# A block substitution emitted in pinned steps, and a longer filler tile, in a hybrid decoder layer

## The chip, the cores and the metric

The kernel runs on one core of a Trainium2 chip. The metric is the device time of one execution in microseconds. The profile calls the engines PE (TensorE), DVE (VectorE), ACT (ScalarE), POOL (GpSimd) and SP (SyncE).

## The reference

One decoder layer on 512 tokens of width 2048, float32:

```python
u = rms_norm(x, norm1_w);  proj = u @ w_in            # 2048 x 6160
conv_out = conformer_conv_group(proj[..., :2048])     # 8 channel groups x 128: GLU, causal depthwise conv (31), LayerNorm, silu
dn_out = gated_deltanet_group(proj[..., 2048:])       # 8 heads x 128, chunked delta rule
h = x + concat(conv_out, dn_out) @ w_out
h = h + square(relu(rms_norm(h, norm2_w) @ w_mlp_up)) @ w_mlp_down   # 2048 -> 8192 -> 2048
y = rms_norm(h, final_norm_w)
```

Inside the delta rule each head needs, for every chunk, the inverse of a unit lower triangular matrix:

```python
a = where(strict, (k_beta @ k.T) * decay, 0)
t_mat = triangular_solve(eye + a, eye, left_side=True, lower=True, unit_diagonal=True)
```

## The kernel before

**Numbers.** Each large product is made of three matmuls (`mm3`, lines 163 to 165): both operands are split into a high part (`hi`, rounded to the fp32r format, a copy on ScalarE) and a low part (`lo`, the rest, a subtraction on VectorE), and high x high, high x low and low x high are added in PSUM. The operand named `lhsT` is the stationary one, of 128 x 128; `rhs` is the moving one, of 128 x 512. In the views of the profile a matmul reads `out<-moving,stationary`.

**Stages.** (1) x is normalised and transposed into `u_h`, `u_l`. (2) The mixers: `ORDER` (line 28) is a list of column tiles. Each letter makes one or more input tiles of 128 columns of `proj` (`in_tile`, results `pin_k`, `pin_q`, ...): K is a head's key tile, C a conv group (two tiles), H a head's query and value tiles (and its gate tile z, if it hasn't been made), Z a gate tile, I the inversion for four heads. I0 serves heads 0 to 3, I1 heads 4 to 7. (3) `w_out` (results `po`), four column blocks. (4) The MLP in 16 blocks of 512: `up_block` (results `pu`, stationary the weights `whi_u`, `wlo_u`, moving the activations) alternates with `down_block` of the block before (results `px`, `py`, stationary the activations `sh`, `sl`, moving the weights `whi_d`, `wlo_d`). (5) The last block's product (`pl`, stationary `hh`, `hl`) and the final norm.

**Order of the mixers.** TensorE goes through the input tiles one after another. The other work of the mixers is written as Python generators, which sit in a list `pending`; every second group of three matmuls in `in_tile` calls `advance()`, which lowers each generator's counter by one and runs it on to its next `yield n` when the counter is used up. An input tile has 16 groups, so 8 advances. So each piece of a head's or a conv group's work is traced behind a certain matmul of a certain tile. In `delta_head` the pauses are `Y_PTQ = 10` until the query is transposed and `rt` is made, `Y_PX2 = 1`, four of `S1 = 1`, eight of `S2 = S3 = 1`, then `osum`, `ors` and `o` (lines 671 to 677), then `Y_POT = 4` until the transposes `pot` (line 681). Heads 0 and 4 take their block inverses later, after `Y_PTQ` and `Y_PX = 4`. In `conv_group` `crs` comes 20 + `Y_CPT` = 34 advances after the start.

Each engine has one queue and takes it in order. The queues' order is fixed before the run by a scheduler, which takes an instruction once it believes its inputs ready, by its own estimates, and of several the one traced first; `ahead()` counts an instruction as traced 600 earlier. `pin` (`tc.keep_in_program_order`) puts an instruction behind the one that was traced before it on the same engine.

**The inversion.** `invert_blocks` (lines 491 to 516) inverts the diagonal blocks of 32 x 32 of four heads at once, on GpSimd: `na` goes to DRAM and comes back as `inv_a`; 31 steps (`j` = 0 to 30) of one multiply (line 511) and one add (line 513) substitute forward; four transfers (line 515) put the result into `blk_out`. It is called at I0 and I1 and is traced there in one piece, 62 compute instructions in a row, none of them pinned. `block_inverse` (line 518) reads it back for a head as `yc` and spreads it into `y` and `xx`.

**Memory.** Tiles take their place in a partition of SBUF pool by pool, in the order in which the pools are opened, each padded to 32 bytes. The pool const begins at byte 16,544 of a partition, actp (`u`, `m`, `v`) at 18,112, wp (the weights) at 83,648, small at 128,704. Its first tile is `small_filler`, which nothing reads or writes. Behind small come rowp (130,592), mixc, inv and tmp; when the mixers are closed, h1p and mlp take their place (mlp from 163,360, with `sh`, `sl`, `hh`, `hl`, and the raw weights `wd`).

Of the kernel before, what the change touches and what calls it, by code (L numbers as in the profile page):

```python
# [8 lines left out]
F32 = mybir.dt.float32  # L9
# [5 lines left out]
P = 128  # L15
SEQ = 512
NT = SEQ // P
# [9 lines left out]
HB = 4  # L27
# [19 lines left out]
def tile_hybrid_block(ctx: ExitStack, tc: tile.TileContext, x, norm1_w, w_in, b_glu, dw_w, dw_b,  # L47
                      ln_g, ln_b, dn_conv_w, a_log, dt_bias, dn_norm_w, w_out, norm2_w, w_up,
                      w_down, final_w, out):
    nc = tc.nc  # L50
# [10 lines left out]
    dram = ctx.enter_context(tc.tile_pool(name="scratch", bufs=2, space=bass.MemoryType.DRAM))  # L61
# [2 lines left out]
    ps_aux = aux_banks.enter_context(tc.tile_pool(name="ps_aux", bufs=4, space=PSUM))  # L64

    small = ctx.enter_context(tc.tile_pool(name="small", bufs=4))
    small.tile([P, 8], F32, tag="small_filler", bufs=1, name="small_filler")

    mixers = ExitStack()
    row_pool = mixers.enter_context(tc.tile_pool(name="rowp", bufs=1))  # L70
# [4 lines left out]
    def tt(tag, name, shape=(P, NT, P), dtype=F32, bufs=1):  # L75
        return tmp.tile(list(shape), dtype, tag=tag, name=name, bufs=bufs)
# [54 lines left out]
    r = 0  # L131
    for v in (norm2_w, b_glu, dw_b, ln_g, ln_b, dn_norm_w):
        n = v.shape[1] // P
# [132 lines left out]
    pin = tc.keep_in_program_order  # L266

    def drain(kind):
        for p in list(pending):
            if p[2].startswith(kind):  # L270
                pending.remove(p)
                for _ in p[0]:
                    pass

    def start(kind, gen):
        drain(kind)
        pending.append([gen, next(gen), kind])
# [13 lines left out]
    def in_weights(col, j, name, sub=nc.vector, first=False):  # L291
        return load_pair(w_in[j * 1024:(j + 1) * 1024, col:col + P]
                         .rearrange("(k p) c -> p k c", p=P), [P, 8, P], f"{name}{j}", sub, first)
# [27 lines left out]
    def decay_products(pabT, toks):  # L321
        for k in range(KT):
            nc.tensor.matmul(pabT[:32, toks], lhsT=ab_w[:, k].rearrange("p a b -> p (a b)"),
                             rhs=uT[k][0][:, toks], start=(k == 0), stop=False)
            nc.tensor.matmul(pabT[:16, toks], lhsT=ab_w[:, k, 0], rhs=uT[k][1][:, toks],
                             start=False, stop=(k == KT - 1))
# [111 lines left out]
    def ahead():  # L438

        return tc.high_priority(offset=600)  # L440
# [49 lines left out]

    def invert_blocks(bt, keys):

        n = HB * NT * 4
        size, step = P * NT * P, 32 * NT * P + 32
        src = dram.tile([HB, 4 * step], F32, tag="blk_in", name=f"blk_in{bt}")
        dst = dram.tile([HB * 4, 32, NT, 32], F32, tag="blk_out", name=f"blk_out{bt}")
        a = inv_pool.tile([n, 32, 32], F32, tag="inv_a", name=f"inv_a{bt}")
        for i, key in enumerate(keys):
            nc.gpsimd.dma_start(src[i, :size].rearrange("(s t c) -> s t c", t=NT, c=P), key[2])
        diag = (src.rearrange("h (b r) -> (h b) r", r=step)[:, :step - 32]  # L500
                .rearrange("q (s t c) -> q t s c", t=NT, c=P)[:, :, :, :32])
        for t in range(NT):
            nc.gpsimd.dma_start(a[t * 4 * HB:(t + 1) * 4 * HB], diag[:, t])
        g = inv_pool.tile([n, 32, 32], F32, tag="inv_g", name=f"inv_g{bt}")
        nc.gpsimd.memset(g, 0.0)
        nc.gpsimd.memset(g.rearrange("n s c -> n (s c)")[:, 0:1024:33], 1.0)
        for j in range(31):
            w = 31 - j
            tm = inv_pool.tile([n, 256], F32, tag="inv_t", bufs=1, name=f"inv_t{bt}_{j}")
            tv = tm[:, :(j + 1) * w].rearrange("n (m i) -> n m i", i=w)  # L510
            nc.gpsimd.tensor_mul(tv, a[:, j:j + 1, j + 1:].to_broadcast([n, j + 1, w]),
                                 g[:, :j + 1, j:j + 1].to_broadcast([n, j + 1, w]))
            nc.gpsimd.tensor_add(g[:, :j + 1, j + 1:], g[:, :j + 1, j + 1:], tv)
        for t in range(NT):
            nc.gpsimd.dma_start(dst[:, :, t], g[t * 4 * HB:(t + 1) * 4 * HB])
        return dst

    def block_inverse(h, blocks):

        y = tt("y", f"y{h}")  # L520
        yc = tt("yc", f"yc{h}", (P, NT, 32))
        b0 = h % HB * 4
        with ahead():
            read = nc.gpsimd.dma_start(yc, blocks[b0:b0 + 4].rearrange("b s t c -> (b s) t c"))
            if h != HB - 1:
                pin(read)
            nc.gpsimd.tensor_mul(y.rearrange("p t (b c) -> p t b c", c=32),
                                 yc.unsqueeze(2).to_broadcast([P, NT, 4, 32]),
                                 block_mask.unsqueeze(1).unsqueeze(3).to_broadcast([P, NT, 4, 32]))


        xx = tt("xx", f"xx{h}")
        with ahead():
            nc.gpsimd.memset(xx, 0.0)
        for block, col in ((0, 0), (2, 32), (0, 64), (1, 96)):
            rows = slice(32 * block, 32 * block + 32)
            pin(nc.vector.transpose(xx[rows, :, col:col + 32], yc[rows]))
        return y, xx

    def delta_head(h, key, blocks, pq, pvv):  # L540
        e_c, e_s, e_l = (eg[:, i, :, h] for i in range(3))
        k, dec, na, kn, br = key
        late = h % HB == 0
        if not late:
            y, xx = block_inverse(h, blocks)
        q = tt("q", f"q{h}")
        short_conv(pq, 0, h, "q", q)
        v = tt("v", f"v{h}")
# [7 lines left out]
        def query_scales():  # L556
            nc.vector.tensor_scalar(ss, ss, EPS, None, ALU.add)
            rt = small.tile([P, NT], F32, tag="rt", bufs=2, name=f"rt{h}")
            with ahead():
                nc.gpsimd.tensor_tensor(rt, ss, neg_half[:, 0:NT], ALU.pow)  # L560
            cq = small.tile([P, 2, NT], F32, tag="cq", bufs=2, name=f"cq{h}")
            nc.vector.tensor_scalar(cq[:, 0], rt, P ** -0.5, None, ALU.mult)
            nc.vector.tensor_mul(cq[:, 1], cq[:, 0], e_c)
            return cq
# [21 lines left out]
        if late:  # L586
            yield Y_PX
            cq = query_scales()
            y, xx = block_inverse(h, blocks)
            yield Y_XX  # L590
        else:
            yield Y_PX2

        for b in (32, 64):
# [3 lines left out]
            for t in range(NT):  # L598
                pin(nc.tensor.matmul(pp[lo:, t], lhsT=na[:m, t, lo:], rhs=xx[:m, t, x0:x0 + 64],
                                     start=True, stop=True))  # L600
# [92 lines left out]
    keys = [None] * NH  # L693
    gates = [None] * NH
    blocks = [None] * (NH // HB)
    for op in ORDER.split():
        kind, r = op[0], int(op[1])
        if kind == "A":

            pabT = ps_mm.tile([P, SEQ], F32, tag="mm", name="pabT")  # L700
            pk = ps_mm.tile([P, SEQ], F32, tag="mm", name="pin_k0")
            ws = [in_weights(C_K, j, "k0", nc.gpsimd, True) for j in range(2)]
            for i in range(2):
                toks = slice(256 * i, 256 * i + 256)
                decay_products(pabT, toks)
                if i:
                    beta, glog_split, eg = decay_columns(pabT)
                for k in range(KT):
                    w = ws[k // 8]
                    mm3(pk[:, toks], (w[0][:, k % 8], w[1][:, k % 8]),  # L710
                        (uT[k][0][:, toks], uT[k][1][:, toks]), start=(k == 0), stop=(k == KT - 1))
        elif kind == "K":
            if r:
                pk = in_tile(C_K + r * P, f"k{r}", nc.gpsimd if r < NPK else nc.vector)
            start(f"key{r}", head_keys(r, pk))
        elif kind == "I":
            drain("key")
            blocks[r] = invert_blocks(r, keys[r * HB:(r + 1) * HB])
        elif kind == "C":
            pa = in_tile(C_CONF + r * P, f"a{r}")  # L720
            start("conv", conv_group(r, pa, in_tile(C_GATE + r * P, f"g{r}")))
        elif kind == "Z":
            drain("head")
            gates[r] = z_gate(in_tile(C_Z + r * P, f"z{r}"), r)
        else:
            pq = in_tile(C_Q + r * P, f"q{r}")
            pvv = in_tile(C_V + r * P, f"v{r}")
            start("head", delta_head(r, keys[r], blocks[r // HB], pq, pvv))
            if gates[r] is None:
                gates[r] = z_gate(in_tile(C_Z + r * P, f"z{r}"), r)  # L730

# [14 lines left out]
    def h1_row(t, dc):  # L746
        return h1[t // 2][dc][:, t % 2]
# [12 lines left out]
    for dc in range(4):  # L760
        ds = slice(dc * 512, (dc + 1) * 512)
        ps = [ps_mm.tile([P, SEQ], F32, tag="mm", name=f"po{dc}{t}") for t in range(NT)]
        for r in range(NH):
            w = load_pair(w_out_v[r, :, :, ds], [P, 2, 512], f"o{dc}{r}")
# [5 lines left out]
            for t in range(NT):  # L770
                cs = slice(t * P, (t + 1) * P)
                for i in range(2):
                    m = mixT[r + NG * i]
                    mm3(ps[t], (m[0][:, cs], m[1][:, cs]), (w[0][:, i], w[1][:, i]),
                        start=(r == 0 and i == 0), stop=(r == NH - 1 and i == 1))
# [176 lines left out]
    for fb in range(NFB):  # L952
        if fb < NFB - 1:
            a = mlp.tile([P, 4, 2, 256], F32, tag="quarters", name=f"a{fb}")
# [31 lines left out]
    for i in range(2):  # L986
        f = w_pool.tile([P, 2, 512], F32, tag="wraw", bufs=3, name=f"fw{i}")
# [5 lines left out]
    for t in range(NT):  # L993
        cs = slice(t * P, (t + 1) * P)
        for dc in range(4):
            ps = ps_mm.tile([P, SEQ], F32, tag="mm", name=f"pl{t}{dc}")
            for k in range(4):
                mm3(ps, (last[k][0][:, cs], last[k][1][:, cs]), last_w[4 * dc + k],
                    start=(k == 0), stop=(k == 3))
            h = h1_row(t, dc)  # L1000
# [6 lines left out]
        for c in (1, 0, 3, 2):  # L1007
            h = h1_row(t, c)
# [33 lines left out]
```

## Time and profile before

| | us |
|---|---|
| median of 3 runs (lowest, highest) | 2228.21 (2224.97, 2228.22) |
| the profiled execution | 2226.59 |
| its span, first to last instruction | 2224.5 |
| TensorE busy in it | 2177.6 |
| VectorE, ScalarE, GpSimd busy | 1527.8, 814.8, 203.1 |

The span is one profiled execution; the profiled execution's own time holds 2.1 us more, around it. Matmuls overlap each other and their durations include their way through the array, so a matmul of 390 ns doesn't keep the next one waiting for as long. What the engine was waiting for is read from the waits and the timelines, and how close matmuls follow each other from their starts.

### The profile page before, as it was taken

The page shows a single profiled execution, that of the slowest core. Times are in us where ns is not written, and L with a number is a line of the kernel's source. Part 1 is how long each engine was busy: PE and PEld are TensorE (multiplying, and loading weights), DVE is VectorE, ACT ScalarE, POOL GpSimd, SP SyncE. Part 2 cuts the span into 40 slices and gives each one's busy share as a digit, 9 for nine tenths or more (in the row PEclk, how much of TensorE's full clock was granted, in tenths as well). Part 3 has the DMA queues.
Part 4 walks back from the last instruction along what each step waited for, and adds up shares of the span by engine and source line. Part 5 has one row for each costly group of instructions (what it writes and reads, how often), then busy time and mean ns, then how long its engine had stood idle before and what let it go on. Part 6 is the DMA issues. An engine that isn't in the chain of part 4 may idle for free.

```text
span 2224.5 us, 25989 instructions
## 1 busy us (share of the span) xinstructions
PE 2177.6 (98%) x10073; PEld 1788.5 (80%) x10073; DVE 1527.8 (69%) x1956; ACT 814.8 (37%) x1349; POOL 203.1 (9%) x265
## 2 busy tenths in 40 slices
PE   6999999989999999999999999999999999999998
PEld 6887888768888788888888888888888888888886
DVE  6658678567668334567767767767767768767775
ACT  5433433423344223323323333333333333333342
POOL 3472102621110000000000000000000000000000
PEclk9999999989999999999999999999999999999999
DMA  5333233322223632233333332332332332333332
GB/s 162 103 98 91 68 88 81 86 73 78 77 78 82 202 96 85 85 105 95 104 105 94 107 106 91 111 107 86 114 104 86 114 104 87 112 104 92 108 123 77
DMA packets 189768, 220.66 MB, mean 99 GB/s; under 512 B 9901, under 2 KB 108622, under 8 KB 189646
## 3 DMA queue, kind: packets, MB, share of 16 engines
q1 hardware_dynamic: 188238, 215.34, 33.4%
q0 software_dynamic: 1408, 3.67, 0.6%
q8 instruction: 79, 1.29, 0.2%
q14 instruction: 43, 0.35, 0.0%
HBM read 212.17 MB, written 6.82 MB: 98 GB/s over the span
## 4 chain that ended last, share of the span: by engine, by line
PE 89%; DVE 5%; POOL 3%; issue 1%; DMA 1%; ACT 1%; SPq 0%; POOLq 0%; DVEq 0%; ACTq 0%
PE pu L164 10%; PE pu L163 10%; PE pu L165 10%; PE px L164 5%; PE px L165 5%; PE px L163 5%; PE py L164 4%; PE py L165 4%; PE py L163 4%; PE po L165 2%; PE po L163 2%; PE po L164 2%; DVE cacc L390 2%; PE pin_a L163 1%; PE pin_a L164 1%
## 5 line engine op out<-in xcount | busy, mean ns | idle before, releaser
L164 PE MATMUL pu<-v_l,whi_u 128*128 128x512 f32 x1024 | 399.6, 390 | 0.0
L163 PE MATMUL pu<-v_h,whi_u 128*128 128x512 f32 x1024 | 399.5, 390 | 0.0
L165 PE MATMUL pu<-v_h,wlo_u 128*128 128x512 f32 x1024 | 399.0, 390 | 0.0
L874 DVE TENSOR_TENSOR wlo_d<-wd,whi_d 128x1024 fp32r<-128x1024 f32 x180 | 218.5, 1220 | 255.3 <-ACT whi_d L873 255.3
L873 ACT CAST whi_d<-wd 128x1024 fp32r<-128x1024 f32 x180 | 188.9, 1049 | 467.5 <-PE pu L164 283.4
L163 PEld LDWEIGHTS pu<-v_h,whi_u 128*128 128x128 f32 x1024 | 192.2, 188 | 42.2 <-issue 0.2
L165 PEld LDWEIGHTS pu<-v_h,wlo_u 128*128 128x128 f32 x1024 | 192.3, 188 | 41.1 <-issue 0.2
L164 PEld LDWEIGHTS pu<-v_l,whi_u 128*128 128x128 f32 x1024 | 192.2, 188 | 40.5
L157 ACT CAST whi_u<-wraw_u 128x1024 fp32r<-128x1024 f32 x128 | 134.6, 1052 | 208.9 <-PE py L165 78.8
L164 PE MATMUL px<-wlo_d,sh 128*128 128x512 f32 x480 | 190.1, 396 | 0.0
L165 PE MATMUL px<-whi_d,sl 128*128 128x512 f32 x480 | 190.1, 396 | 0.0
L163 PE MATMUL px<-whi_d,sh 128*128 128x512 f32 x480 | 190.0, 396 | 0.0
L390 DVE SCALAR_TENSOR_TENSOR cacc<-chh,dw_cols,cacc 128x511 f32<-128x511 f32 (+14 forms) x240 | 180.7, 753 | 6.1 <-ACT cacc L387 2.7
L158 DVE TENSOR_TENSOR wlo_u<-wraw_u,whi_u 128x1024 fp32r<-128x1024 f32 x128 | 155.9, 1218 | 41.4 <-ACT whi_u L157 41.4
L891 DVE TENSOR_TENSOR h<-px,h 128x1024 f32<-128x1024 f32 x120 | 146.6, 1222 | 34.1 <-PE px L165 33.9
L164 PE MATMUL py<-wlo_d,sh 128*128 128x512 f32 x360 | 142.6, 396 | 0.0
L165 PE MATMUL py<-whi_d,sl 128*128 128x512 f32 x360 | 142.6, 396 | 0.0
L163 PE MATMUL py<-whi_d,sh 128*128 128x512 f32 x360 | 142.5, 396 | 0.0
L891 DVE TENSOR_TENSOR h<-py,h 128x1024 f32<-128x1024 f32 x90 | 110.1, 1223 | 28.6 <-PE py L165 26.8
L176 POOL TENSOR_TENSOR rs_rf<-rs_sf,neg_half 128x1 f32<-128x1 f32 x4 | 2.2, 542 | 1331.0 <-DVE rs_sf L174 1331.0
L165 PEld LDWEIGHTS px<-whi_d,sl 128*128 128x128 f32 x480 | 90.3, 188 | 21.8
L164 PEld LDWEIGHTS px<-wlo_d,sh 128*128 128x128 f32 x480 | 90.4, 188 | 21.7
(304 smaller groups left out, 4099.9 us busy)
## 6 DMA issues: line engine op xcount, KB each, us to landing
wraw_u<-in_w_mlp_up SPq DMA_DIRECT2D x128, 512.0 KB, 3.7
wd<-in_w_mlp_down SPq DMA_DIRECT2D x120, 512.0 KB, 3.7
wraw_o<-in_w_out SPq DMA_DIRECT2D x32, 512.0 KB, 4.3
wraw_k<-in_w_in SPq DMA_DIRECT2D x16, 512.0 KB, 4.0
wraw_z<-in_w_in SPq DMA_DIRECT2D x16, 512.0 KB, 4.0
wraw_a<-in_w_in SPq DMA_DIRECT2D x16, 512.0 KB, 4.0
wraw_g<-in_w_in SPq DMA_DIRECT2D x16, 512.0 KB, 3.9
wraw_q<-in_w_in SPq DMA_DIRECT2D x16, 512.0 KB, 4.0
```

Source lines behind the costliest of these rows:

```text
L157: nc.scalar.copy(hi, raw)
L158: sub.tensor_sub(lo, raw, hi.bitcast(F32))
L163: nc.tensor.matmul(ps, lhsT=sta[0], rhs=mov[0], start=start, stop=False, skip_group_check=more)
L164: nc.tensor.matmul(ps, lhsT=sta[0], rhs=mov[1], start=False, stop=False, skip_group_check=more)
L165: nc.tensor.matmul(ps, lhsT=sta[1], rhs=mov[0], start=False, stop=stop, skip_group_check=more)
L176: nc.gpsimd.tensor_tensor(rr, s, neg_half[:, 0:1], ALU.pow)
L390: nc.vector.scalar_tensor_tensor(acc[:, j:], hh[:, :SEQ - j], dw_cols[:, WCONV - 1 - j, g:g + 1], acc[:, j:], ALU.mult, ALU.add)
L873: nc.scalar.copy(hi, src)
L874: nc.vector.tensor_sub(lo, src, hi.bitcast(F32))
L891: nc.vector.tensor_add(h, ps, h)
```

## The change

`invert_blocks` becomes a generator that is put into `pending` like the others: it pauses 6 advances after its loads, then runs one step at a time, with a pause of 1 advance after each, or of 2 after every even step from 6 to 24. Each multiply and add is pinned. `block_inverse` drains the generator before the first head of a batch reads its result. `small_filler` grows from 8 to 48 floats, from 32 to 192 bytes in each partition.

```diff
-    small.tile([P, 8], F32, tag="small_filler", bufs=1, name="small_filler")
+    small.tile([P, 48], F32, tag="small_filler", bufs=1, name="small_filler")
...
-        dst = dram.tile([HB * 4, 32, NT, 32], F32, tag="blk_out", name=f"blk_out{bt}")
+        dst = blocks[bt] = dram.tile([HB * 4, 32, NT, 32], F32, tag="blk_out", name=f"blk_out{bt}")
...
         nc.gpsimd.memset(g.rearrange("n s c -> n (s c)")[:, 0:1024:33], 1.0)
+        yield 6
         for j in range(31):
...
-            nc.gpsimd.tensor_mul(tv, a[:, j:j + 1, j + 1:].to_broadcast([n, j + 1, w]),
-                                 g[:, :j + 1, j:j + 1].to_broadcast([n, j + 1, w]))
-            nc.gpsimd.tensor_add(g[:, :j + 1, j + 1:], g[:, :j + 1, j + 1:], tv)
+            pin(nc.gpsimd.tensor_mul(tv, a[:, j:j + 1, j + 1:].to_broadcast([n, j + 1, w]),
+                                     g[:, :j + 1, j:j + 1].to_broadcast([n, j + 1, w])))
+            pin(nc.gpsimd.tensor_add(g[:, :j + 1, j + 1:], g[:, :j + 1, j + 1:], tv))
+            yield 2 if j % 2 == 0 and 6 <= j < 25 else 1
...
-    def block_inverse(h, blocks):
+    def block_inverse(h):
...
+        if h % HB == 0:
+            drain("blocks")
...
-            blocks[r] = invert_blocks(r, keys[r * HB:(r + 1) * HB])
+            start("blocks", invert_blocks(r, keys[r * HB:(r + 1) * HB]))
```

## Rows read from the trace of the kernel before

**Rows 1.** What TensorE waited for, 0 to 800: total us, times, longest.

```profile
PE pot L681 <- POOL o L677: 13.7, 2, 13.1
```

**Rows 2.** Two stretches: length, busy us and instructions of each engine, clock, DMA.

```profile
455.00:458.00 3.00, 3.00 (x10) 2.42 (x9) 2.15 (x3) 0.24 (x1) 0.00 (x0) 0.50 0.00 0
...
890.00:2150.00 1260.00, 1260.00 (x5470) 1027.70 (x5469) 907.83 (x886) 446.99 (x561) 0.00 (x0) 1.00 0.34 101
```

**Rows 3.** Timeline of TensorE around 441: start, us, engine, line, operation.

```profile
440.97 0.39 PE L165 MATMUL pin_q<-u_h,wlo_q 128*128 128x512 f32 x1
...
454.47 1.11 PE L681 MATMUL pot<-ident,o 128*128 128x128 f32 x4 [13.11 <-POOL o L677]
```

**Rows 4.** Timeline of GpSimd, second batch.

```profile
412.00 1.03 POOL L560 TENSOR_TENSOR rt<-dss,neg_half 128x4 f32<-128x4 f32 x1
...
442.81 0.85 POOL L513 TENSOR_TENSOR inv_g<-inv_g,inv_t 64x175 f32<-64x175 f32 x1
...
451.90 1.05 POOL L676 TENSOR_TENSOR ors<-osum,neg_half 128x4 f32<-128x4 f32 x1
...
491.79 0.65 POOL L524 DMA_DIRECT2D yc<-blk_out  x1
```

**Rows 5.** Timeline of VectorE before 441.

```profile
436.79 0.52 DVE L673 TENSOR_SCALAR osum<-osum 128x4 f32<-128x4 f32 x1 [0.53 <-ACT oj L445]
```

**Rows 6.** Large matmuls by line: count, busy us, mean ns, idle time before them.

```profile
L163 PE MATMUL pu<-v_h,whi_u 128*128 128x512 f32 x1024 | 399.5, 390 | 0.0
...
L163 PE MATMUL px<-whi_d,sh 128*128 128x512 f32 x480 | 190.0, 396 | 0.0
...
L163 PE MATMUL py<-whi_d,sh 128*128 128x512 f32 x360 | 142.5, 396 | 0.0
...
L164 PE MATMUL po<-wlo_o,m_h 128*128 128x512 f32 x256 | 100.0, 391 | 0.0
...
L163 PE MATMUL pl<-wl_h,hh 128*128 128x512 f32 x64 | 25.4, 396 | 0.0
```

**Rows 7.** Timeline of TensorE around 1400, first and last of two runs.

```profile
1399.84 0.39 PE L163 MATMUL px<-whi_d,sh 128*128 128x512 f32 x1
...
1401.71 0.39 PE L165 MATMUL px<-whi_d,sl 128*128 128x512 f32 x1
...
1401.94 0.39 PE L163 MATMUL pu<-v_h,whi_u 128*128 128x512 f32 x1
...
1407.18 0.39 PE L165 MATMUL pu<-v_h,wlo_u 128*128 128x512 f32 x1
```

**Rows 8.** Timeline of GpSimd, first batch.

```profile
119.57 0.23 POOL L511 TENSOR_TENSOR inv_t<-inv_a,inv_g 64x31 f32<-64x31 f32 x1
...
150.82 0.62 POOL L511 TENSOR_TENSOR inv_t<-inv_a,inv_g 64x240 f32<-64x240 f32 x1
...
151.40 1.03 POOL L488 TENSOR_TENSOR kn<-kss,half 128x4 f32<-128x4 f32 x1
...
173.11 0.59 POOL L513 TENSOR_TENSOR inv_g<-inv_g,inv_t 64x31 f32<-64x31 f32 x1
...
178.92 0.95 POOL L505 MEMSET inv_g<- 64x1024 f32 x1 [2.38 <-DMA blk_out<-inv_g]
...
192.75 0.63 POOL L524 DMA_DIRECT2D yc<-blk_out  x1
...
200.31 1.03 POOL L408 TENSOR_TENSOR crs<-vs,neg_half 128x4 f32<-128x4 f32 x1 [4.24 <-DVE vs L405]
```

**Rows 9.** Timeline of VectorE near 130.

```profile
130.45 0.43 DVE L473 TENSOR_SCALAR kss<-kss 128x4 f32<-128x4 f32 x1
```

**Rows 10.** A group of small matmuls.

```profile
L619 PE MATMUL pw<-y,kg 128*128 128x128 f32 x64 | 8.4, 274 | 0.0
```

**Rows 11.** Page, costliest groups: two subtractions of VectorE.

```profile
L874 DVE TENSOR_TENSOR wlo_d<-wd,whi_d 128x1024 fp32r<-128x1024 f32 x180 | 218.5, 1220 | 255.3 <-ACT whi_d L873 255.3
...
L158 DVE TENSOR_TENSOR wlo_u<-wraw_u,whi_u 128x1024 fp32r<-128x1024 f32 x128 | 155.9, 1218 | 41.4 <-ACT whi_u L157 41.4
```

More of the change, by code (lines that the diff above doesn't have):

```diff
@@ L510, in invert_blocks @@
             tv = tm[:, :(j + 1) * w].rearrange("n (m i) -> n m i", i=w)
-            nc.gpsimd.tensor_mul(tv, a[:, j:j + 1, j + 1:].to_broadcast([n, j + 1, w]),
-                                 g[:, :j + 1, j:j + 1].to_broadcast([n, j + 1, w]))
-            nc.gpsimd.tensor_add(g[:, :j + 1, j + 1:], g[:, :j + 1, j + 1:], tv)
+            pin(nc.gpsimd.tensor_mul(tv, a[:, j:j + 1, j + 1:].to_broadcast([n, j + 1, w]),
+                                     g[:, :j + 1, j:j + 1].to_broadcast([n, j + 1, w])))
+            pin(nc.gpsimd.tensor_add(g[:, :j + 1, j + 1:], g[:, :j + 1, j + 1:], tv))
+            yield 2 if j % 2 == 0 and 6 <= j < 25 else 1
         for t in range(NT):
             nc.gpsimd.dma_start(dst[:, :, t], g[t * 4 * HB:(t + 1) * 4 * HB])
-        return dst
-    def block_inverse(h, blocks):
+    def block_inverse(h):
         y = tt("y", f"y{h}")
         yc = tt("yc", f"yc{h}", (P, NT, 32))
+        if h % HB == 0:
+            drain("blocks")
         b0 = h % HB * 4
         with ahead():
-            read = nc.gpsimd.dma_start(yc, blocks[b0:b0 + 4].rearrange("b s t c -> (b s) t c"))
+            read = nc.gpsimd.dma_start(yc, blocks[h // HB][b0:b0 + 4].rearrange("b s t c -> (b s) t c"))
             if h != HB - 1:
@@ L538, in block_inverse, with delta_head @@
         return y, xx
-    def delta_head(h, key, blocks, pq, pvv):
+    def delta_head(h, key, pq, pvv):
         e_c, e_s, e_l = (eg[:, i, :, h] for i in range(3))
@@ L544, in delta_head @@
         if not late:
-            y, xx = block_inverse(h, blocks)
+            y, xx = block_inverse(h)
         q = tt("q", f"q{h}")
@@ L588, in delta_head @@
             cq = query_scales()
-            y, xx = block_inverse(h, blocks)
+            y, xx = block_inverse(h)
             yield Y_XX
@@ L727, in tile_hybrid_block @@
             pvv = in_tile(C_V + r * P, f"v{r}")
-            start("head", delta_head(r, keys[r], blocks[r // HB], pq, pvv))
+            start("head", delta_head(r, keys[r], pq, pvv))
             if gates[r] is None:
```

## The prediction

> **What bounds the kernel now.** I read the page's busy shares first: TensorE is busy for 2177.6 of 2224.5 us, so time is won only where it waits or where its matmuls stand too far apart. Then the list of what TensorE waited for. After the start one entry is large: the transposes of `pot` waited 13.1 us once for GpSimd's `o` [rows 1]. The timeline of TensorE puts it at H3: the last matmul before it starts at 440.97, the transposes at 454.47 [rows 3]. One matmul takes 0.23 of that, so 13.3 us are lost there. Behind it the granted clock is 0.50 of full for 3 us [rows 2], 1.2 instead of 2.4 GHz, which costs about another 1.5 us.
>
> The timeline of GpSimd says why. `osum`, from which `ors` is made, is done on VectorE at 437.3 [rows 5]; `ors` starts at 451.90, when the 31 substitution steps of the second batch and their four transfers have been through GpSimd's queue [rows 4]. GpSimd takes its queue in order, and in this order `ors` stands last.
>
> For the other 1260 us, from 890 to 2150, TensorE has no idle time at all [rows 2]. There only the distance between matmuls counts, and the groups by line show two kinds. All are 128 rows by 512 columns in the same number format, yet those of `pu` and `po` take 390 and 391 ns and those of `px`, `py` and `pl` 396 [rows 6]. The durations overlap, so I took starts from the timeline: eight steps of `px` in 1.87 us are 233.8 ns each, 23 of `pu` in 5.24 us are 227.8 [rows 7]. Both views say 6 ns. What the slow kind has in common is the stationary operand: `sh`, `sl`, `hh` or `hl`, all from the mlp pool. The moving operand doesn't do it (`px` moves `whi_d` of wp and `po` moves `whi_o` of wp), nor does the bank (`pl` and `po` both write ps_mm).
>
> **The change part by part.** *The steps of the second batch.* They are unchanged in number and size (62 instructions of GpSimd in a batch), so no engine gets more work. What changes is the order. A step is now traced at an advance, of which each input tile has eight, and pinned behind the GpSimd instruction traced before it. I counted advances from I1: step 0 at 6, steps 1 to 6 at 7 to 12, then two steps in three advances up to step 24 at 39, steps 25 to 30 at 41 to 46, the transfers at 47. H3's head starts at 16; `rt` is traced at 16 + 10 = 26; then come 1 + 4 + 8 = 13 advances to `ors` and `o` at 39, and 4 to `pot` at 43. H4's first tile begins at advance 40, and three advances into it is where the trace has `pot`, so the count holds. At 39 the substitution comes before the head in `pending`, so step 24 is traced ahead of `ors`, and step 25 is pinned behind `o`. Whatever the scheduler believes, six steps and the four transfers must now follow `o`.
>
> Do the other 25 still precede it? The scheduler takes `ors` when it believes it ready, and it believes GpSimd faster than it is. In the first batch `kn` of K5 could run from 130.9, when `kss` was done [rows 9], but stands in the queue behind the multiply of step 17, at 151.40 [rows 8]. So 17 steps that took from 119.57 to 150.82, 1.84 us each, were believed to fit into 11.3 us, 0.7 each. In the second batch `rt` stands behind step 5, at 412.00 [rows 4]; from there to `osum` at 437.3 are 25 us, and steps 6 to 24 need 19 x 0.7 = 13 by that belief. So I take it that all 25 precede. Nothing before them moves, so step 24 ends as now, at 442.81 + 0.85 = 443.66 [rows 4], and `ors` starts there instead of at 451.90: 8.2 us earlier, and `pot` with it. The bounds: at most the whole 13.3, had `ors` come ahead of the rest; at least 5, if the start of the batch comes some 3 us later through a different order of its loads. The shorter wait, about 5 us, may or may not still cost the slow clock; I take that it does, so nothing from there, with 1.5 as the other end. After `pot` comes VectorE's `mix`, which waits for it now too; GpSimd's last six steps then end near 452, and their transfers are needed by H4's read of `yc`, now at 491.79 [rows 4] and then some 8 us earlier, so 30 us remain.
>
> *The steps of the first batch.* They keep GpSimd about as long. The first result is needed by the read of `yc` at 192.75; the result had landed by 178.92, when the next memset could start [rows 8]. That is 13.8 us of cover, and steps may slip by so much at no cost. `kn`, before the steps or among them, feeds nothing of this stretch. I take 0; beyond the cover each us would cost one.
>
> *The filler.* It is 160 bytes longer, so every pool behind it begins 160 bytes later. The mlp pool now starts at byte 163,360 of a partition, 32 past a multiple of 64; then at 163,520, a multiple. Modulo 512 it goes from 32 to 192, which is where act and wp stand now. So the stationary tiles of `px`, `py` and `pl` come to lie, to any power of two up to 512, as those of `po` do. If the start address makes the 6 ns, 3 x (480 + 360 + 64) = 2712 matmuls give 2712 x 6 = 16.3 us. Bounds: 0, if it is something else about that pool, and 7 ns each, 19.0 us, if the timeline's figures are rounded against it. I take 16.3, since `pl` against `po` leaves little else that differs.
>
> The same shift moves rowp, mixc, inv and tmp, so the stationary tiles of some 1,100 small matmuls and transposes (10073 less the large ones of all kinds), such as `pw` [rows 10]. None of this form has a stationary tile on a multiple of 64 now. Its bounds are 0 and the 6 ns of the large ones, 6.6 us; I take 1 ns each, 1.1 us, near the lower end, because they run in chains that wait for other engines. `ab_w` alone goes the other way, from a multiple of 64 to 32 past one: 64 matmuls, 0.4 us at most. On VectorE the start seems not to matter: `wlo_d` from a raw tile in mlp takes 1220 ns, `wlo_u` from one in wp 1218 [rows 11], so I take 0, and at most 180 x 2 ns.
>
> **The sum.** The profiled execution took 2226.6 us, 1.6 below the median of the runs shown (2224.97 to 2228.22). 2226.6 - 8.2 - 16.3 - 1.1 = 2201.0.
>
> **The rivals.** *The filler does nothing* (12 in 100). The 6 ns may belong to the pool for another reason: where its tiles lie, or how they are written. For it: no row shows one tile at two addresses. Against it: `sh` and `m_h` are made in the same way, by a copy on ScalarE, and `sl` and `m_l` by a subtraction on VectorE. It gives 2226.6 - 8.2 = 2218.4. The Trainium skill speaks for this rival: "SBUF — State Buffer", Specifications, gives cachelines of 16 bytes, and both starts are multiples of 16, so by that page neither operand would be dearer and the sum would be 2218.4; it names no coarser line, and the two kinds of matmul in this trace are something that it doesn't explain.
>
> *The whole stall goes* (13 in 100): the scheduler believes the steps slower than I read, and `ors` comes ahead of most. Then the slow clock goes too: 2226.6 - 13.3 - 1.5 - 17.4 = 2194.4.
>
> *The stall stays and the filler works* (7 in 100): the pins don't do what the change says, or another instruction is late at the same place: 2226.6 - 17.4 = 2209.2.
>
> *Neither works* (4 in 100): 2226.6.
>
> *Slower* (4 in 100): steps of the first batch come to stand behind C0's `crs`, which waits for VectorE until 200.31 [rows 8]. The cover of 13.8 us and the gain of 25.6 must be used up: the batch, whose last add ends at 173.7 now, would end about 173.7 + 13.8 + 25.6 = 213, so it decides from some nine steps of 1.3 us behind `crs`. With thirteen of them the batch ends near 218 and it gives about 2232. Against it: by the count the last step is traced 47 advances after I0, and C0's `crs` at 40 + 34 = 74.
>
> **How the numbers follow.** My forecast, both parts as in the sum, has 60 in 100, with 2195 to 2207 as its own range: below by the 5.5 us that the small matmuls may give beyond my 1.1, above by the 3 us of the loads and 2.7 if the slow kind falls by 5 ns only. Of the rivals, the whole stall and the filler alone lie at 2194 and 2209, so 2190 to 2214 holds 80 in 100; the lower end leaves room for part of the 19.0 and 6.6. Outside stay the idle filler, no change and the slower case. A measurement of this kernel tells about 0.2%, 4.5 us, from no change. Faster by more: 60 + 12 + 13 + 7 = 92. Within: 4. Slower: 4.
>
> **What would show it.** In the trace of the changed kernel: the wait of `pot` for `o` near 5 us instead of 13.1; `ors` behind the second add of 64x175 and ahead of six more steps; the groups of `px`, `py` and `pl` at 390 ns and not 396, with starts 228 ns apart; `pu` and `po` as they were; the read of `yc` for H0 not later after `rt` than now. Wrong it would be if `px` stays at 396 (8 to 12 us short), if `pot` still waits 13, or if a new wait of TensorE for GpSimd shows up near H0 or H4.

## The result

| | before | after |
|---|---|---|
| median (lowest, highest), runs | 2227.74 (2224.97, 2228.22), 4 | 2199.36 (2198.72, 2200.43), 4 |
| the profiled execution | 2226.59 | 2199.81 |
| its span | 2224.5 | 2197.8 |
| TensorE busy in it | 2177.6 | 2157.8 |

The ratio is 0.9876, with a 95% interval of 0.9859 to 0.9893: the changed kernel is faster by 1.1 to 1.4%. The forecast was 2201.0, in a range of 2190 to 2214. In the changed kernel the lines behind the inversion are 4 higher (`pot` L685, `ors` L680, `o` L681).

### The profile after

The list of what TensorE waited for, 0 to 800 (total us, times, longest), against [rows 1]:

```profile
PE pot L685 <- POOL o L681: 5.6, 2, 5.0
...
PE cpb L416 <- DVE chn L411: 2.3, 1, 2.3
```

The wait at H3 went from 13.1 to 5.0 us. The timeline of GpSimd (start, us, engine, line, operation) shows why, against [rows 4]:

```profile
444.75 0.85 POOL L515 TENSOR_TENSOR inv_g<-inv_g,inv_t 64x175 f32<-64x175 f32 x1
445.55 0.52 POOL L538 MEMSET xx<- 128x512 f32 x1
446.03 1.01 POOL L680 TENSOR_TENSOR ors<-osum,neg_half 128x4 f32<-128x4 f32 x1
447.12 1.04 POOL L681 TENSOR_TENSOR o<-o,ors 128x512 f32<-128x512 f32 x1
448.12 0.49 POOL L513 TENSOR_TENSOR inv_t<-inv_a,inv_g 64x156 f32<-64x156 f32 x1
...
455.46 0.72 POOL L515 TENSOR_TENSOR inv_g<-inv_g,inv_t 64x31 f32<-64x31 f32 x1
456.48 1.95 POOL L518 DMA_DIRECT2D blk_out<-inv_g  x3 [0.29 <-POOL inv_g L515]
```

`ors` stands behind the add of 64x175, which is step 24, and `o` ahead of the multiply of 64x156, which is step 25: the place that was counted from the advances. The clearing of `xx`, part of the next head's `block_inverse`, stands ahead of `ors` now. In the kernel before it stood between `ors` and `o`, and cost as much there:

```profile
452.90 0.52 POOL L534 MEMSET xx<- 128x512 f32 x1
453.39 1.03 POOL L677 TENSOR_TENSOR o<-o,ors 128x512 f32<-128x512 f32 x1
```

The starts of TensorE's matmuls give the sizes. Timeline of the changed kernel, against [rows 3, 7]:

```profile
439.01 0.39 PE L163 MATMUL pin_q<-u_h,whi_q 128*128 128x512 f32 x1
...
442.86 0.39 PE L165 MATMUL pin_q<-u_h,wlo_q 128*128 128x512 f32 x1
448.21 1.12 PE L685 MATMUL pot<-ident,o 128*128 128x128 f32 x4 [4.96 <-POOL o L681]
...
458.13 0.39 PE L163 MATMUL pin_v<-u_h,whi_v 128*128 128x512 f32 x1
...
932.34 0.39 PE L163 MATMUL px<-whi_d,sh 128*128 128x512 f32 x1
...
1397.46 0.39 PE L163 MATMUL px<-whi_d,sh 128*128 128x512 f32 x1
...
1399.95 0.39 PE L165 MATMUL px<-whi_d,sl 128*128 128x512 f32 x1
1400.18 0.39 PE L163 MATMUL pu<-v_h,whi_u 128*128 128x512 f32 x1
...
1405.39 0.39 PE L165 MATMUL pu<-v_h,wlo_u 128*128 128x512 f32 x1
...
2145.46 0.39 PE L163 MATMUL pl<-wl_h,hh 128*128 128x512 f32 x1
```

And four starts of the kernel before that were not shown yet:

```profile
437.10 0.40 PE L163 MATMUL pin_q<-u_h,whi_q 128*128 128x512 f32 x1
...
463.62 0.39 PE L163 MATMUL pin_v<-u_h,whi_v 128*128 128x512 f32 x1
...
937.01 0.39 PE L163 MATMUL px<-whi_d,sh 128*128 128x512 f32 x1
...
2171.11 0.40 PE L163 MATMUL pl<-wl_h,hh 128*128 128x512 f32 x1
```

The gap ahead of `pot`, start to start, was 454.47 - 440.97 = 13.50 and is 448.21 - 442.86 = 5.35, 8.15 less. The whole query tile of H3, up to the first `pin_v`, took 26.52 and takes 19.12, 7.40 less. The MLP from the first `px` to the first `pl` took 1234.1 and takes 1213.1, 21.0 less. Eleven steps of `px` in 2.49 us are 226 ns each now, as 23 of `pu` in 5.21 are.

The groups by line (count, busy us, mean ns, idle time before) say it of all of them, against [rows 6, 10]:

```profile
L163 PE MATMUL pu<-v_h,whi_u 128*128 128x512 f32 x1024 | 398.4, 389 | 0.0
L163 PE MATMUL px<-whi_d,sh 128*128 128x512 f32 x480 | 186.7, 389 | 0.0
L163 PE MATMUL py<-whi_d,sh 128*128 128x512 f32 x360 | 140.0, 389 | 0.0
L163 PE MATMUL pl<-wl_h,hh 128*128 128x512 f32 x64 | 25.0, 391 | 0.0
L623 PE MATMUL pw<-y,kg 128*128 128x128 f32 x64 | 8.4, 274 | 0.0
```

`px` and `py` fell from 396 to 389, to the level of `pu`; the small `pw` stayed at 274. Four stretches (length, busy us of TensorE, weight loads, VectorE, ScalarE, GpSimd, then the granted clock), against [rows 2]; the second begins with `pot`:

```profile
203.00:215.00 12.00, 11.53 (x71) 9.20 (x72) 6.82 (x14) 5.56 (x9) 0.00 (x0) 0.86 0.27 75
...
448.21:453.70 5.49, 5.49 (x15) 4.52 (x16) 3.28 (x4) 1.05 (x1) 4.86 (x9) 0.50 0.00 0
453.70:458.13 4.43, 4.43 (x21) 3.59 (x20) 4.25 (x7) 0.03 (x1) 3.90 (x7) 1.00 0.61 133
890.00:2150.00 1260.00, 1260.00 (x5559) 1042.86 (x5558) 925.42 (x913) 460.47 (x582) 0.00 (x0) 1.00 0.34 103
```

In the same 1260 us of the MLP TensorE starts 5559 matmuls and not 5470: 226.7 ns each on average and not 230.3. Behind the shorter wait the clock is still granted at half, 1.2 and not 2.4 GHz, until 453.70.

### The profile page after: what moved, and what is told of

Its sections match the earlier page's. It is cut to its first block, busy times and chain, and to the rows that moved or that the text cites. A ratio compares the mean times of both kernels' runs of the same rounds, so it can differ in the third digit from the quotient of the medians.

```text
span 2197.8 us, 25990 instructions
## 1 busy us (share of the span) xinstructions
PE 2157.8 (98%) x10073; PEld 1788.0 (81%) x10073; DVE 1525.2 (69%) x1956; ACT 815.6 (37%) x1349; POOL 212.4 (10%) x265
## 4 chain that ended last, share of the span: by engine, by line
PE 87%; DVE 7%; POOL 3%; issue 2%; ACT 1%; DMA 1%; SPq 0%; POOLq 0%; DVEq 0%; ACTq 0%
PE pu L165 10%; PE pu L163 10%; PE pu L164 10%; PE px L165 5%; PE px L164 5%; PE px L163 5%; PE py L165 4%; PE py L164 4%; PE py L163 4%; DVE cacc L390 3%; PE po L165 2%; PE po L163 2%; PE po L164 2%; PE pin_g L163 1%; PE pin_g L164 1%
## 5 line engine op out<-in xcount | busy, mean ns | idle before, releaser
L163 PEld LDWEIGHTS px<-whi_d,sh 128*128 128x128 f32 x480 | 90.1, 188 | 18.7
```

Source lines behind the costliest of these rows:

```text
L163: nc.tensor.matmul(ps, lhsT=sta[0], rhs=mov[0], start=start, stop=False, skip_group_check=more)
```

## The experiments

All times are medians, and each ratio is to the kernel before as it ran on the same chip: 2228.6 (8 runs) beside the first four, 2226.8 (9 runs) beside the weights moved, all moved, the ladder and the two advances, 2227.1 (7 runs) beside the other two. "Between starts" is the mean distance from a matmul's start to the start of the next one, worked out from all distances under 300 ns. Every edit is to the changed kernel, but for the first.

**The filler alone**, in the kernel before.

```diff
-    small.tile([P, 8], F32, tag="small_filler", bufs=1, name="small_filler")
+    small.tile([P, 48], F32, tag="small_filler", bufs=1, name="small_filler")
```

> The kernel before with the filler of 192 bytes alone; the substitution stays in one piece. My theory (a stationary tile that starts on a multiple of 64 bytes saves 6 to 7 ns a large matmul, whatever the order): px, py and pl at 389 ns, starts 227 ns apart, pot still waits 13 us, and the time is 2227.7 less about 19 to 22, so 2204 to 2209 us. Rival (the faster matmuls of the changed kernel come with its other order, not with the addresses): px, py and pl stay at 396 and the time at 2227 us.

Measured: 2206.5, ratio 0.9903 (0.9889 to 0.9918). `px`, `py` and `pu` are 226.7 ns between starts, `pl` 226.8; the gap ahead of `pot` stays at 13.54.

**The steps alone**: the changed kernel with the filler of before.

```diff
-    small.tile([P, 48], F32, tag="small_filler", bufs=1, name="small_filler")
+    small.tile([P, 8], F32, tag="small_filler", bufs=1, name="small_filler")
```

> The changed kernel with the filler back at 32 bytes; the steps stay pinned among the tiles. My theory (the steps give what the wait of pot loses, and nothing else): pot waits about 5 us, px, py and pl at 396 ns, 2227.7 - 8.2 = 2219.5 us (2217 to 2222). Rival (the order also speeds the matmuls of the MLP): 389 ns and below 2210 us.

Measured: 2219.8, ratio 0.9964 (0.9951 to 0.9977). `px` and `py` are 233.9 ns between starts, the gap ahead of `pot` is 5.27. The filler is worth 22.1 us and the steps 8.8, together 30.9, against 28.4 for both in the comparison above. The 2.5 us between them lie within the intervals, so nothing shows that the parts touch each other.

**A filler of 64 bytes.** The mlp pool then starts at 64 modulo 512 (64 bytes past a multiple of 512): a multiple of 64, but not where act and wp stand, at 192.

```diff
-    small.tile([P, 48], F32, tag="small_filler", bufs=1, name="small_filler")
+    small.tile([P, 16], F32, tag="small_filler", bufs=1, name="small_filler")
```

> The changed kernel with a filler of 64 bytes: the pools behind it start on a multiple of 64 again, but at 64 past a multiple of 512 instead of 192. If a multiple of 64 is what counts: px, py and pl at 389 ns and 2199 us (2197 to 2202). If the tiles must stand as those of act and wp do modulo 256 or 512: 396 ns and about 2221 us.

Measured: 2215.9, ratio 0.9948 (0.9933 to 0.9963). The groups by line:

```profile
L163 PE MATMUL pu<-v_h,whi_u 128*128 128x512 f32 x1024 | 398.4, 389 | 0.0
L163 PE MATMUL px<-whi_d,sh 128*128 128x512 f32 x480 | 189.9, 396 | 0.0
```

`px` is at 396 again, 232.9 between starts. A multiple of 64 isn't enough. `pu` is at 389 in this group, yet not as in the changed kernel: it is 227.3 between starts, against 226.7 there and 227.6 before.

**No pins.** The steps are traced in pieces at the same advances, but the scheduler is free to order them.

```diff
-            pin(nc.gpsimd.tensor_mul(tv, a[:, j:j + 1, j + 1:].to_broadcast([n, j + 1, w]),
-                                     g[:, :j + 1, j:j + 1].to_broadcast([n, j + 1, w])))
-            pin(nc.gpsimd.tensor_add(g[:, :j + 1, j + 1:], g[:, :j + 1, j + 1:], tv))
+            nc.gpsimd.tensor_mul(tv, a[:, j:j + 1, j + 1:].to_broadcast([n, j + 1, w]),
+                                 g[:, :j + 1, j:j + 1].to_broadcast([n, j + 1, w]))
+            nc.gpsimd.tensor_add(g[:, :j + 1, j + 1:], g[:, :j + 1, j + 1:], tv)
```

> The changed kernel without the pins: the steps are traced at the same advances, with the same pauses. My theory (the scheduler believes GpSimd faster than it is and takes every step that nothing holds back, so only the pin behind o keeps six of them behind ors): the queue has all 31 steps before ors again, pot waits about 13 us and the time is 2199.4 + 8.2 = 2207.6 us (2205 to 2210). Rival (the place in the trace is enough, the later steps have lower priority): pot waits 5 us, 2199 us.

Measured: 2205.1, ratio 0.9907 (0.9889 to 0.9924); the gap ahead of `pot` is 13.66. Timeline of GpSimd:

```profile
447.35 0.26 POOL L515 TENSOR_TENSOR inv_g<-inv_g,inv_t 64x31 f32<-64x31 f32 x1
...
450.31 0.64 POOL L518 DMA_DIRECT2D blk_out<-inv_g  x1
450.95 1.05 POOL L680 TENSOR_TENSOR ors<-osum,neg_half 128x4 f32<-128x4 f32 x1
```

`ors` stands behind the last step (64x31) and the transfers again. The place in the trace alone moves nothing: the wait is as long as with the filler alone (13.54), so the pins carry the whole gain of the steps.

**The weights moved against the rest.** A tile of 32 bytes ahead of the weights puts wp at 224 modulo 512; a filler 32 bytes shorter keeps mlp at 192, where act stands.

```diff
+    w_pool.tile([P, 8], F32, tag="w_shift", bufs=1, name="w_shift")
...
-    small.tile([P, 48], F32, tag="small_filler", bufs=1, name="small_filler")
+    small.tile([P, 40], F32, tag="small_filler", bufs=1, name="small_filler")
```

> The changed kernel with 32 bytes more ahead of the weight tiles in wp and 32 fewer in the filler: wp goes to 224 modulo 512, act and mlp stay at 192. In px and po the weights move and the activations stand, in pu and pin the weights stand. If the stationary tile's own address counts: px and po stay at 389 to 391 ns, pu and pin go to 395 or more, which costs some 5300 x 6 = 32 us. If the two operands must stand alike: all four are slow, some 8600 x 6 = 52 us, near 2250. If the moving tile's own address counts: px and po slow, pu and pin as they were, 2220.

Measured: 2242.5 (2 runs), ratio 1.0072 (1.0054 to 1.0090): slower than before. The groups by line, whose lines are one higher here:

```profile
L164 PE MATMUL pu<-v_h,whi_u 128*128 128x512 f32 x1024 | 405.3, 396 | 0.0
L164 PE MATMUL px<-whi_d,sh 128*128 128x512 f32 x480 | 189.4, 395 | 0.0
L164 PE MATMUL pl<-wl_h,hh 128*128 128x512 f32 x64 | 24.9, 389 | 0.0
```

`pu`, `px`, `py` and `po` are all 233.2 to 233.4 ns between starts. `pl` alone stays near 227, and it alone has neither operand in wp: it moves `wl_h` and `wl_l` of act, and its stationary `hh` and `hl` lie in mlp. `pu` has its stationary operand in wp and its moving one in act, `px` and `po` the other way round. That is how it must be if what counts is that the two stand differently. By itself this run would also fit a rule that a tile off a multiple of 64, as those of wp are here, is slow; the filler of 64 bytes and the ladder below are slow on multiples of 64 too, where only the distance is left. In size it is 43 us against the changed kernel, where 52 were expected if all four are slow.

**All moved together**: 64 bytes more ahead of act, so that act, wp and mlp stand at 256 modulo 512.

```diff
-    const.tile([P, 8], F32, name="const_filler")
+    const.tile([P, 24], F32, name="const_filler")
```

> The changed kernel with 64 bytes more at the very start: act, wp and mlp all go from 192 to 256 modulo 512 and stand alike as now. If the operands must stand alike: all large matmuls stay at 389 to 390 ns and the time at 2199 us. If 192 itself is the good place (by the tile's own address, 64 was bad and 256 is unknown): some or all at 395, 2215 to 2260 us.

Measured: 2196.4 (2 runs), ratio 0.9865 (0.9847 to 0.9883). `px`, `py` and `pu` are at 226.7, `pl` at 226.8 (`px` at 389 by its group). So 192 is no special place.

**A ladder of offsets.** The stationary tiles of a down block's seven products are set 0, 32, 96, 64, 128, 160 and 192 bytes off from the moving ones.

```diff
         def split(src, i):
+            if i and not fb:
+                mlp.tile([P, 8], F32, tag=f"step{i}", name=f"step{i}")
             hi = mlp.tile([P, 2, 256], F32R, tag=f"sh{i}", name=f"sh{fb}_{i}")
```

> The changed kernel with 32 bytes put in ahead of each of the seven pairs of stationary tiles but the first: the products of a down block, in the order 0 to 6, then have their stationary tile 0, 32, 96, 64, 128, 160 and 192 bytes further than the moving one, modulo 512. If standing alike counts: product 0 at 227 ns between starts, and those that are off slower, 4 as in the run with the filler of 64 (there the offset was -128), 5 or 2 as before the change (-160) if the pattern repeats after 512 or 256. If a threshold in the offset counts, the step between fast and slow is seen on the way. If the offset doesn't matter: all seven at 227 or all at one other figure.

Measured: 2214.2 (1 run). First and last starts of three of the products in one block, the first, second and seventh:

```profile
1261.60 0.39 PE L163 MATMUL px<-whi_d,sh 128*128 128x512 f32 x1
...
1264.09 0.40 PE L165 MATMUL px<-whi_d,sl 128*128 128x512 f32 x1
1264.33 0.39 PE L163 MATMUL py<-whi_d,sh 128*128 128x512 f32 x1
...
1266.89 0.40 PE L165 MATMUL py<-whi_d,sl 128*128 128x512 f32 x1
...
1294.70 0.39 PE L163 MATMUL px<-whi_d,sh 128*128 128x512 f32 x1
...
1297.22 0.39 PE L165 MATMUL px<-whi_d,sl 128*128 128x512 f32 x1
```

Eleven steps take 2.49, 2.56 and 2.52 us: 226, 233 and 229 ns. Within one execution and one loop it is the distance between the two tiles that was set apart. Over all blocks, without the step from one product to the next:

| stationary tile behind the moving one, bytes | ns between starts |
|---|---|
| 0 | 226.7 |
| 32 | 232.9 |
| 64 | 233.3 |
| 96 | 234.3 |
| 128 | 233.0 |
| 160 | 233.3 |
| 192 | 229.5 |

Counted in the same way, the kernel before, at -160, has 234.2, and the filler of 64 bytes, at -128, 233.0. Both fit the ladder if it repeats after 256 bytes: -160 is then 96 and -128 is 128.

**A step of 256 bytes** ahead of the second pair only.

```diff
         def split(src, i):
+            if i == 1 and not fb:
+                mlp.tile([P, 64], F32, tag="step", name="step")
             hi = mlp.tile([P, 2, 256], F32R, tag=f"sh{i}", name=f"sh{fb}_{i}")
```

> The changed kernel with a tile of 256 bytes ahead of the second of the seven pairs of stationary tiles, so that in the first of the seven products of a down block the stationary tile stands like the moving one, and in the other six (2160 of the 2520 matmuls of px and py) 256 bytes off, modulo 512. If what counts repeats after 256 bytes, as the ladder's products at +128 and +160 suggest, all seven stay 226.7 ns apart and the time is that of the changed kernel, about 2199. If it repeats only after 512 or more, the six are between 230 and 234 ns apart and the time is 2199 + 2160 x 3 to 7 ns, 2206 to 2214; the first product stays at 226.7 in both cases.

Measured: 2197.1 (1 run), all seven products at 226.67. So a distance of 256 bytes is as good as none. A stretch of this run that the last section comes back to:

```profile
203.00:215.00 12.00, 12.00 (x80) 9.91 (x80) 9.03 (x15) 5.94 (x10) 0.00 (x0) 1.00 0.17 46
```

**Two advances for every step from 6 on**, so that more of the steps fall behind `ors` and `o`.

```diff
-            yield 2 if j % 2 == 0 and 6 <= j < 25 else 1
+            yield 2 if j >= 6 else 1
```

> The changed kernel with a pause of two advances after every step from step 6 on: by the count step 19 is the last ahead of ors. My theory (ors stands behind as many steps as are traced ahead of it, and GpSimd has done 20 of them when osum is ready): ors starts without a wait in the queue, pot waits under 1 us, the slow clock behind it goes too, 2199.4 - 5.1 - 1.5 = about 2193 us (2191 to 2195). Rival (the wait only moves, since the later steps now delay the transfers or H4's y): pot no longer waits but pp or y does, and the time stays at 2198 to 2201.

Measured: 2191.7 (2189.3 to 2194.1, 5 runs), ratio 0.9843 (0.9830 to 0.9857). GpSimd and then TensorE:

```profile
435.75 0.71 POOL L515 TENSOR_TENSOR inv_g<-inv_g,inv_t 64x240 f32<-64x240 f32 x1
436.40 0.52 POOL L538 MEMSET xx<- 128x512 f32 x1
438.26 1.01 POOL L680 TENSOR_TENSOR ors<-osum,neg_half 128x4 f32<-128x4 f32 x1 [1.34 <-DVE osum L677]
439.35 1.04 POOL L681 TENSOR_TENSOR o<-o,ors 128x512 f32<-128x512 f32 x1
```

```profile
438.30 0.39 PE L163 MATMUL pin_q<-u_h,whi_q 128*128 128x512 f32 x1
...
442.15 0.39 PE L165 MATMUL pin_q<-u_h,wlo_q 128*128 128x512 f32 x1
442.38 0.60 PE L685 MATMUL pot<-ident,o 128*128 128x128 f32 x4
...
449.67 0.39 PE L163 MATMUL pin_v<-u_h,whi_v 128*128 128x512 f32 x1
```

GpSimd waits for `osum` now and not the other way round, TensorE doesn't wait for `o`, and the clock stays up (1.00 from 442 to 450). H3's query tile takes 11.37 us. This is the whole stall: against 26.52 it was worth 15.15 us, of which 13.27 was the wait (13.50 less the 0.23 that one matmul takes) and 1.9 the slow clock behind it.

**Both**: two advances, and all moved by 64 bytes.

```diff
-    const.tile([P, 8], F32, name="const_filler")
+    const.tile([P, 24], F32, name="const_filler")
...
-            yield 2 if j % 2 == 0 and 6 <= j < 25 else 1
+            yield 2 if j >= 6 else 1
```

> Two edits that have each been run alone: a pause of two advances from step 6 on (2191.7), and everything from act on moved by another 64 bytes together (2196.4, 3.0 below the changed kernel). If the 3.0 came from the place of the tiles, the two add up: 2188.7. If it came only from a shorter start of that execution, as its profile has it (by 439 it is 3.6 us ahead of the changed kernel, and all matmuls stand as close), this is 2191.7 again, within 2.

Measured: 2189.1 (2186.3 to 2190.3, 4 runs), ratio 0.9825 (0.9809 to 0.9842): the fastest of all, by 38.0 us against the kernel before. It lies at the end of the range where the two edits add up, but its intervals overlap with those of two advances alone, and the profile doesn't put the difference on the place of the tiles: `px`, `py` and `pu` are at 226.7 in both, and this execution is 2.7 us ahead when H3's query tile starts, mostly for the reason in the last section. Whether the second move gives anything stays open.

## Why the prediction was right, and where it wasn't

**The stall: right, mechanism and size.** 8.2 us were forecast and 8.15 measured, by the order that the text gave: step 24, `ors`, `o`, step 25. All 25 steps precede, as the reading of the scheduler had it. One count in that reading was off: the multiply of 64x240 ahead of `kn` in the first batch [rows 8] is that of step 19 and not 17, so 19 steps, 1.64 us each, were believed to fit into 11.3 us, 0.6 each. That makes the belief faster still, and the conclusion stands. The run without pins shows that nothing but the pins puts `o` ahead of the rest. In absolute time step 24 ended at 445.60 and not at 443.66, since this execution was 1.9 us later at that point. The clearing of `xx` put `ors` another 0.4 later, but it no longer stands between `ors` and `o`: from the start of `ors` to `pot` are 2.18 us and not 2.57, so the two cancel.

**The clock behind it: right that it still falls, but not at the same price.** It fell after 5 us as after 13, and the text took no gain from there. Against the run with two advances the tile lost 19.12 - 11.37 = 7.75 us, 5.12 of it the wait (5.35 less 0.23), so 2.6 are left for the slow clock, where before it was 1.9. The granted clock bears this out: TensorE works at half from 448.21 to 453.70, and in the kernel before from 454.47 to 458.34.

```profile
454.47:458.34 3.87, 3.87 (x11) 3.23 (x12) 2.15 (x3) 0.58 (x1) 0.00 (x0) 0.50 0.00 0
```

Half of 5.49 is 2.7 us, half of 3.87 is 1.9. That is why the tile gained 7.40 and not 8.15. The price isn't fixed: with the filler of 64 bytes and with the step of 256 the gap is 5.35 too, but the tile takes 17.95 and 17.86 us, 1.4 to 1.5 for the clock.

**The filler: right place and sign, a little too small, and the wrong rule.** The step that failed is that the start address of the stationary tile makes the 6 ns, a multiple of 64 being the good one. The filler of 64 bytes made such a start and the matmuls stayed slow. The observation beside it held: the tiles come to stand where act and wp stand. The runs show that neither place matters by itself (all moved: fast; weights alone moved: slow), only the distance between the stationary and the moving tile of a matmul, modulo 256 bytes. In the kernel before `px`, `py` and `pl` had 32 - 192 = -160, in the changed one 0. `pu` and `po` had 0 in both.

In size: 2712 matmuls at 6 ns gave 16.3. Between starts it is 233.9 - 226.7 = 7.2 ns for `px` and `py`, 18.2 us, and `pl` brings 1.1: 19.3 in all, a little above the upper bound of 19.0. Another 2.8 us came from `pu`, whose 3072 matmuls went from 227.6 to 226.7 ns although neither operand moved.

Both misses have one source. A start of the kernel before shows it, beside the first and the last `pu` in [rows 7]:

```profile
1403.10 0.39 PE L165 MATMUL pu<-v_h,wlo_u 128*128 128x512 f32 x1
```

The stretch of 24 `pu` that begins at 1401.94 behind `px` takes 1.16 us for its first five steps, 232 ns each, and 4.08 for the other 18, 226.7 each. Over all stretches the first five steps are 230.8, 235.8, 228.3, 232.5 and 230.9 ns and the rest 226.7: 2.6 of the 2.8 us lie there. So the 23 steps of `pu` that gave 227.8 held five slow ones, which raise their mean by 1.1 ns, and the difference to `px` came out that much too small. `pu` follows its slow neighbours: the steps alone leave it at 227.6, the filler of 64 bytes, with `px` a little less slow, brings 227.3 and only three slow first steps, and in the ladder a stretch of `pu` loses nothing behind the product at 0 and 38 ns behind the one at 160, in the same execution. It doesn't behind each of them (nothing behind the one at 96), and what in the chip carries over isn't shown.

**The small matmuls: nothing, where 1.1 was taken.** `pw` is 274 before and after. Its two operands `y` and `kg` both lie behind small and moved together, so by the rule above their distance didn't change; that reason is argued, and no run took it apart.

**The first batch: right at nothing.** The result had landed by 182.87, when the next clearing of `inv_g` could start, and `yc` is read at 194.42, directly behind `rt`, as before.

**The sum.** By the profiled executions 2226.6 - 2199.8 = 26.8: H3's query tile 7.4, the MLP from `px` to `pl` 21.0, `pl` 1.0 (44.7 to 43.7 by its first and last start), less 1.9 that were lost ahead of 439 and 0.8 between that tile and the MLP. The forecast had 25.6, in another mixture: 3.0 too little for `px`, `py` and `pl`, 2.8 for `pu` missing, 1.1 for small matmuls too much, and 3.5 of small losses that it didn't have (0.8 in the tile, 1.9 and 0.8). That the sum came so near is in part luck: 5.8 us too little and 4.6 too much.

**The rivals.** That the filler does nothing is refuted. Its support from the Trainium skill, "SBUF — State Buffer", Specifications, with cachelines of 16 bytes, gives no difference between these starts, all multiples of 16; the ladder shows 226.7 to 234.3 ns among them, and the measurement decides. That the whole stall goes was false for this change, but its price of 14.8 was near: two advances a step make it go, for 15.15.

## What to carry to other kernels

Let the stationary and the moving tile of a matmul like these (128x128 by 128x512, fp32r) start at the same place modulo 256 bytes: here 7 of 234 ns hung on it, and a tile that nobody reads buys it. To see such a cost, compare the distance between starts of products of one shape, not busy times, and leave out the first steps behind another product, which can carry its cost; to find its rule, set several distances inside one kernel. All the pairs shown to be fast here stood on multiples of 64; two tiles that stand alike off such a multiple were not run. And a long chain on an engine with an order written out by hand must be cut and pinned so that the short, urgent instruction stands ahead of its rest; how many pieces stand ahead is a number to try, since two advances in place of one and a half gave nearly as much again.

## What the runs showed of the hardware

The distance rule was not expected: 226.7 ns at 0 and at 256 bytes, 232.9 to 234.3 from 32 to 160, 229.5 at 192, and 233.2 at 224 (`px` and `py` with the weights moved, -32).

The clock behind a short wait isn't the same in every execution. At H0 TensorE waits 2.0 to 2.5 us for `chn` in all of them but the one with the weights moved (0.7). In the 12 us behind it the granted clock was 0.86 in the changed kernel and 1.00 in the run with the step of 256 bytes, as the two rows of 203 to 215 show; it was 0.89 in the kernel before, 0.87 with two advances, 0.86 in the ladder and 0.76 with the filler of 64 bytes, but 1.00 with all moved, with both, without pins, with the filler alone and with the steps alone. The wait doesn't tell them apart: start to start, the gap was 2.47 in the kernel before, where the clock fell, and 2.84 with the steps alone, where it didn't. From the query tile at H0 to the value tile behind it takes 21.7 to 22.1 us with the slow clock (23.5 with the filler of 64 bytes) and 20.0 to 20.5 without. The step of 256 bytes and the ladder touch only the MLP, far behind this place, and still stand on the two sides. So two single profiles can differ by 1.5 us there for no edit that was made, and the first gate tile begins anywhere from 115.3 to 117.8 us: together as much as some of the effects above.
